# Feed-forward blocks of an encoder trunk: the hand-ordered steps begin at the third pair instead of the fourth, and nine of eleven pairs use seven block products instead of eight

## The chip, the core and the metric

The kernel runs on one core of a Trainium2 chip. A core has five engines, each with its own instruction queue: TensorE (PE in the profile, with its weight loads listed apart as PEld), VectorE (DVE), ScalarE (ACT), GpSimd (POOL) and SyncE (SP), which here only issues DMAs. Engines wait for each other through semaphores. Matmul results go to PSUM, of which this kernel uses eight banks of 128 x 512 fp32; everything else lives in SBUF. The metric is the device time of one launch in microseconds.

## The reference

The reference is a two-layer encoder trunk on 512 tokens of width 1024. Each layer has a feed-forward block, a token mixer (neighbourhood attention in layer 0, a bidirectional RWKV-7 scan in layer 1) and a second feed-forward block, each with a residual and a layer norm. The change touches the four feed-forward blocks only:

```python
def swiglu(x, w_in, w_out):
    gate, up = jnp.split(x @ w_in, 2, axis=-1)
    return (jax.nn.silu(gate) * up) @ w_out

for i in range(DEPTH):                                   # DEPTH = 2
    x = layer_norm(DN_ALPHA * x + 0.5 * swiglu(x, ffn_w_in[i, 0], ffn_w_out[i, 0]), ...)
    ...                                                  # mixer and its norm
    x = layer_norm(DN_ALPHA * x + 0.5 * swiglu(x, ffn_w_in[i, 1], ffn_w_out[i, 1]), ...)
```

`w_in` is 1024 x 5632, `w_out` is 2816 x 1024, all in fp32.

## The kernel before, in words

**Precision.** Every fp32 operand is kept as a high part `h` (rounded to the matmul's format) and a low part `l`. `split` (L278) makes them: ACT copies raw to `h` (L280), DVE or POOL subtracts `h` from raw (L281). A product is three matmuls: h·h, h·l, l·h.

**Tiles of the feed-forward block.** The 2816 hidden columns are NF = 22 tiles of 128, numbered f = 0 to 21, and taken in 11 pairs c: pair c holds f = 2c and f = 2c + 1. For each f there is a gate block and an up block of `w_in`. `ffn` (L465) walks over the pairs; `gated` (L519) makes silu(gate) · up / 2 with one ACT instruction (Silu, L522) and one DVE instruction (L523); `posts` (L525) forms sums and differences of the pair's four quarter tiles with DVE (L529 to L532) and splits them; `sums` (L1128) loads two row tiles of `w_out` and forms sums of them (L1135 to L1140) and splits (tile `wx`); `early` (L1183) multiplies the previous pair's results with these into six PSUM banks (L1206, 18 matmuls of 128 x 512 a pair).

**Two ways to do an input tile.** The plain way is `proj` (L294 with L290 to L292) or, in the hand-ordered part, `plain` (L1065): gate and up, each 8 blocks of 128 input channels by 3 matmuls of 512 columns, 48 matmuls of 128 x 512 for one f. The other way, `products` (L1075), takes gate and up of one f together as a two-by-two block matrix, the tokens' two halves as the other side, and does seven block products in place of eight, Strassen's way in Winograd's form: 7 x 12 = 84 matmuls of 128 x 256. It costs sums on both sides. Those of the weights are made by `weights` (L1013) for each such f with four more DVE instructions (L1040, L1041, L1044, L1048), and eleven half-size splits per pair, seven for the odd f and four for the plain even f. Those of the tokens are made once per block by `mixes` (L944), in four parts, into the four tiles of `right`.

**Which pairs use which.** `SEVEN` (L84) lists the odd f that are done by seven products. A pair whose odd f is in it is built by `slot` (L979), under `manual_schedule` for PE, ACT and DVE: within the slot the instructions of these three engines stand in the order in which the code issues them, and `FF_SEQ` (L86) deals them out among the threads g (plain), s (products), e (early), w (weights), k (posts), u and z (w_out sums). Pairs before that are laid out by the tile scheduler, which picks each engine's order from its own timeline; it may also place scheduled instructions among the first hand-ordered ones. `MIXED` (L85) lists the f after whose `gated` each part of `mixes` is issued.

**What ties the first slot to what stands before it.** All f from 2 on share two PSUM banks, `own` (L933): the gate goes to the first, the up to the second, so the next gate waits for Silu (ACT, L522) to have read the first and the next up waits for L523 (DVE) to have read the second. `prepare` (L994), called while the last plain f before `SEVEN` is projected (L497 to L504), runs the first six steps of `weights`, so that the first slot finds its units. The weights arrive through two `raw` buffers of 128 x 1024; a new load of a buffer waits until the DVE subtraction that last read it is done. All DMAs are issued by SP in one queue.

```python
for c in range(npairs):                                   # ffn, L479
    if 2 * c + 1 in SEVEN:                                # L481
        with self.tc.manual_schedule(engines=MANUAL_SCAN):
            raw = seven.slot(c, out, pool, posts)
    ...
            first = f + 2 == SEVEN[0]                     # L497
            if first:
                seven.prepare(4)
    ...
        if f in MIXED:                                    # L506
            seven.mixes(MIXED.index(f))
```

Of the kernel before, what the change touches and what calls it, by code (L numbers as in the profile page):

```python
# [23 lines left out]
NF = FF // P  # L24
# [56 lines left out]
EARLY_TAGS = ("kz1", "v", "vr", "qc", "qd", "zs", "qs", "tm")  # L81
DECAY = math.exp(-0.5)
GN_EPS = 64e-5
SEVEN = range(7, NF, 2)  # L84
MIXED = (0, 1, 2, 4)  # L85
FF_SEQ = ("g k z u w g w w k g w k g k g s w s w s e e e w s w s s u s s u s s u s e s w s e e w u")  # L86


# [21 lines left out]
class Trunk:  # L110
# [354 lines left out]
    def ffn(self, xT, w_in, w_out, ln, nxt, lead=None):  # L465
# [10 lines left out]
        with self.pool("fa") as pool:  # L476
# [3 lines left out]
            for c in range(npairs):  # L480
                if 2 * c + 1 in SEVEN:  # L481
                    with self.tc.manual_schedule(engines=MANUAL_SCAN):
# [8 lines left out]
                for j in range(2):  # L491
# [3 lines left out]
                    elif not pps:  # L495
                        us = self.units if f == 1 else [self.load_cols(w_in, FF * i + f * P, eng=nc.vector) for i in range(2)]
                        first = f + 2 == SEVEN[0]  # L497
                        if first:
# [6 lines left out]
                    self.gated(pps.pop(0), pps.pop(0), raw[:, 3:7:3] if j else raw[:, 0:8:7])  # L505
                    if f in MIXED:  # L506
                        seven.mixes(MIXED.index(f))
                    if c and j == 0:
# [412 lines left out]
class Seven:  # L921
# [57 lines left out]
    def slot(self, c, out, pool, posts):  # L979

        if 2 * c + 3 not in SEVEN:
            self.work = chain(self.work, out.opening())
# [3 lines left out]
        for name in FF_SEQ.split():  # L986
            next(threads[name], None)
        if 2 * c + 3 not in SEVEN:
            list(out.third(c))
# [23 lines left out]
    def weights(self):  # L1013
# [4 lines left out]
        r = [h for raw in (k.raw(), k.raw()) for h in (raw[:, :512], raw[:, 512:])]  # L1018
        pairs = list(SEVEN)

# [1174 lines left out]
```

## Time and profile before

| | us |
|---|---|
| three runs | 2142.55, 2145.98, 2149.44 (median 2145.98) |
| the profiled execution, its own time | 2143.44 |
| its span, first to last instruction | 2141.7 |
| TensorE clock granted over the span | 0.999 |

The four feed-forward blocks are called FFN0 to FFN3 below. In the profiled execution their first slots begin at 87.6, 671.2, 1018.1 and 1864.5 us from the span's start. In a row of the timeline the first number is the start, the second how long the merged group took, then engine, line, operation, output tile<-input tiles, shape and count; brackets hold the engine's idle time before the row and what ended it. Matmuls overlap, so the step from start to start is the cost of one, not its duration.

### The profile page before, as it was taken

What the parts mean: (1) busy time and instruction counts of PE and PEld (TensorE: products, weight loads), DVE (VectorE), ACT (ScalarE), POOL (GpSimd) and SP (SyncE); (2) the same over time, 40 slices, a digit from 0 to 9 for tenths busy, and PEclk for the clock granted to TensorE, in tenths of its full rate; (3) what the DMA queues carried; (4) which work ended last, traced back from release to release, by engine and by line L of the source; (5) the groups of instructions that cost most, each with busy time, mean ns of one, the idle gap of its engine ahead of it and who ended that gap; (6) DMA issues with size and microseconds to landing.
All of it is one profiled execution on the core that took longest, in us unless ns stands there. A gap on an engine that the chain in (4) does not pass through costs nothing.

```text
span 2141.7 us, 39209 instructions
## 1 busy us (share of the span) xinstructions
PE 2114.4 (99%) x15104; PEld 1715.0 (80%) x15104; DVE 1572.5 (73%) x2678; ACT 1081.1 (50%) x2119; POOL 403.3 (19%) x622
## 2 busy tenths in 40 slices
PE   9999999999999999999999999999999999999998
PEld 8888888888788888888888887535777667788886
DVE  7677776277486777788777779835898658777776
ACT  4444445367443444454444543636888534445443
POOL 1000003455310000020000013043788710000000
PEclk9999999999999999999999999999999999999999
DMA  6544494342334444935444764773454651545474
GB/s 194 186 164 158 158 349 145 111 126 84 99 118 158 158 158 159 388 116 173 138 158 158 276 244 129 270 241 113 115 147 123 223 193 64 169 144 176 169 279 171
DMA packets 180972, 369.44 MB, mean 173 GB/s; under 512 B 34384, under 2 KB 54480, under 8 KB 178736
## 3 DMA queue, kind: packets, MB, share of 16 engines
q1 hardware_dynamic: 180784, 366.94, 50.4%
q8 instruction: 118, 1.93, 0.4%
q14 instruction: 70, 0.57, 0.1%
HBM read 286.13 MB, written 68.68 MB: 166 GB/s over the span
## 4 chain that ended last, share of the span: by engine, by line
PE 77%; DVE 12%; ACT 7%; issue 2%; DMA 1%; POOL 0%; SPq 0%; ACTq 0%; DVEq 0%; POOLq 0%
PE bank L1062 18%; PE bank L1206 17%; PE bank L291 6%; PE bank L290 6%; PE bank L292 5%; PE a L1397 5%; PE bank L353 4%; DVE wx L281 2%; PE g L1723 2%; DVE w L281 1%; ACT ring L280 1%; ACT w L280 1%; PE y L1397 1%; DVE ring L281 1%; PE bank L1590 1%
## 5 line engine op out<-in xcount | busy, mean ns | idle before, releaser
L280 ACT ACTIVATE w<-raw 128x512 fp32r<-128x512 f32 (+1 forms) x302 | 215.0, 727 | 236.9 <-DVE raw L1041 53.9
L1062 PE MATMUL bank<-xT,w 128*128 128x512 f32 (+1 forms) x1572 | 303.2, 347 | 1.3
L1062 PEld LDWEIGHTS bank<-xT,w 128*128 128x128 f32 x1572 | 254.9, 189 | 46.3 <-ACT tmp L522 9.7
L281 DVE TENSOR_TENSOR w<-raw,w 128x512 fp32r<-128x512 f32 (+1 forms) x272 | 206.4, 766 | 86.6 <-ACT w L280 85.5
L447 POOL COPY marks<-x 128x1 f32<-128x1 f32 x8 | 8.2, 1026 | 1039.4 <-DVE x L439 1037.9
L1206 PE MATMUL bank<-wx,an 128*128 128x512 f32 x792 | 200.8, 392 | 0.0
L1206 PE MATMUL bank<-w,ring 128*128 128x512 f32 x720 | 169.2, 390 | 0.0
L280 ACT ACTIVATE ring<-raw 128x512 fp32r<-128x512 f32 (+1 forms) x147 | 102.1, 705 | 119.5 <-DVE raw L1041 37.2
L1206 PEld LDWEIGHTS bank<-wx,an 128*128 128x128 f32 x792 | 142.5, 189 | 24.9
L1206 PEld LDWEIGHTS bank<-w,ring 128*128 128x128 f32 x720 | 135.0, 188 | 29.1 <-DVE w L281 0.3
L290 PE MATMUL bank<-xT,w 128*128 128x512 f32 x368 | 145.1, 394 | 2.4 <-DVE ar L523 2.4
L291 PE MATMUL bank<-xT,w 128*128 128x512 f32 x368 | 143.5, 390 | 0.0
L292 PE MATMUL bank<-xT,w 128*128 128x512 f32 x368 | 142.8, 389 | 0.0
L1062 PE MATMUL bank<-xT,ring 128*128 128x512 f32 (+1 forms) x732 | 140.9, 345 | 0.5
L1062 PEld LDWEIGHTS bank<-xT,ring 128*128 128x128 f32 x732 | 118.0, 189 | 20.4 <-ACT tmp L522 3.8
L1062 PE MATMUL bank<-ring,w 128*128 128x256 f32 x960 | 127.8, 283 | 0.0
L1062 PEld LDWEIGHTS bank<-ring,w 128*128 128x128 f32 x960 | 123.2, 191 | 3.3
L1832 POOL TENSOR_TENSOR tm<-qs,zs 128x126 f32<-128x126 f32 (+22 forms) x248 | 109.6, 442 | 61.4 <-DVE qs L1825 24.0
L1834 POOL TENSOR_TENSOR zs<-zs,tm 128x126 f32<-128x126 f32 (+22 forms) x248 | 108.6, 438 | 19.4
L281 DVE TENSOR_TENSOR ring<-raw,ring 128x512 fp32r<-128x512 f32 (+1 forms) x123 | 85.6, 700 | 25.7 <-ACT ring L280 25.4
L281 DVE TENSOR_TENSOR wx<-ra,wx 128x512 fp32r<-128x512 f32 x132 | 87.2, 686 | 7.5 <-ACT wx L280 4.4
L281 POOL TENSOR_TENSOR w<-raw,w 128x1024 fp32r<-128x1024 f32 x30 | 74.1, 2475 | 86.7 <-ACT w L280 80.7
(386 smaller groups left out, 4555.4 us busy)
## 6 DMA issues: line engine op xcount, KB each, us to landing
raw<-in_ffn_w_in_dram SPq DMA_DIRECT2D x256, 256.0 KB, 3.8
ra<-in_ffn_w_out_dram SPq DMA_DIRECT2D x44, 1024.0 KB, 5.0
raw<-in_ffn_w_in_dram SPq DMA_DIRECT2D x48, 512.0 KB, 3.8
d_away<-away SPq DMA_DIRECT2D x44, 512.0 KB, 4.1
ring<-d_away SPq DMA_DIRECT2D x16, 1024.0 KB, 10.3
xT<-d_late SPq DMA_DIRECT2D x29, 512.0 KB, 9.2
xT<-in_ffn_w_out_dram SPq DMA_DIRECT2D x27, 512.0 KB, 7.9
d_late<-ts SPq DMA_DIRECT2D x44, 256.0 KB, 3.8
```

Of the source, the lines that this page charges most:

```text
L280: self.hi = self.nc.scalar.activation(h, raw, AF.Copy).ins
L281: self.lo = (eng or self.nc.vector).tensor_tensor(l, raw, h.bitcast(F32), ALU.subtract).ins
L290: nc.tensor.matmul(out, wh, xh, start=start, stop=False)
L291: nc.tensor.matmul(out, wh, xl, start=False, stop=False)
L292: nc.tensor.matmul(out, wl, xh, start=False, stop=stop)
L353: nc.tensor.matmul(acc[t, h], a, u[:, i, h * 512 : (h + 1) * 512], start=first and n == 0, stop=last and n == 2)
L1062: self.nc.tensor.matmul(out, w[:, i, cs], x(c)[j], start=start and c + n == 0, stop=stop and c == 3 and n == 2, skip_group_check=True)
L1206: self.nc.tensor.matmul(acc, lhs, u[:, i], start=bool(first) and m == 0, stop=last and m == 2, skip_group_check=more)
L1397: self.nc.tensor.matmul(out[hs], w[:, hs], x, start=start, stop=stop)
L1723: nc.tensor.matmul(pgs[h][:, j * P : (j + 1) * P], flat(bk[hs, q * 4 + j]), ar[hs, :, q * 4 + j], start=True, stop=True)
L1832: nc.gpsimd.tensor_tensor(tv, qs[:, s, 0:s].rearrange("p (a o) -> p a o", o=1).broadcast_to([P, s, n]), zs[:, s : s + 1, c0:].broadcast_to ...
L1834: nc.gpsimd.tensor_tensor(zs[:, 0:s, c0:], zs[:, 0:s, c0:], tv, ALU.add)
```

## The change

`SEVEN` begins at f = 5 instead of 7, so pair 2 (f = 4 and 5) is done by a slot, and there are nine slots instead of eight. The last part of the token mixes is issued after f = 3 instead of f = 4. `prepare` follows by itself: it now runs while f = 3 is projected instead of f = 5.

```diff
-SEVEN = range(7, NF, 2)
-MIXED = (0, 1, 2, 4)
+SEVEN = range(5, NF, 2)
+MIXED = (0, 1, 2, 3)
```

Outside the feed-forward blocks every engine's order is the same as before. FFN1, FFN2 and FFN3 are laid out alike on ACT and DVE; FFN0 differs a little.

**PE in FFN0, from the end of f = 3's gate.** `bank_441` is the gate's bank, `bank_442` the up's; `w_523` and `w_528` are f = 3's gate and up weights; the L1206 rows are the matmuls of `early`. Before, f = 3's up follows its gate at once:

```order
L1206 MATMUL bank_515<-wx_280,an_402 128x512
L292 MATMUL bank_441<-xT_93,w_523 128x512
L290 MATMUL bank_441<-xT_93,w_523 128x512
L291 MATMUL bank_441<-xT_93,w_523 128x512
L292 MATMUL bank_441<-xT_93,w_523 128x512
L290 MATMUL bank_442<-xT_92,w_528 128x512
```

In the changed kernel the first slot's gate matmuls (L1062, weights `ring_260`) stand between them:

```order
L1206 MATMUL bank_514<-wx_280,an_402 128x512
L1206 MATMUL bank_515<-wx_280,an_402 128x512
L1062 MATMUL bank_441<-xT_92,ring_260 128x512 x12
L1062 MATMUL bank_441<-xT_93,ring_260 128x512 x11
L290 MATMUL bank_442<-xT_92,w_528 128x512
```

And where f = 3's up ends, one gate matmul is left before the slot's up (`ring_261`, `w_547`), which writes the same `bank_442`; the 128x256 rows are the first two of the seven products:

```order
L292 MATMUL bank_442<-xT_93,w_528 128x512
L1062 MATMUL bank_441<-xT_93,ring_260 128x512
L1062 MATMUL bank_442<-xT_92,ring_261 128x512 x12
L1062 MATMUL bank_442<-xT_93,w_547 128x512 x12
L1062 MATMUL bank_441<-xT_92,w_547 128x256 x12
L1062 MATMUL bank_441<-ring_256,w_579 128x256 x12
```

What moved: 23 of the slot's first 24 matmuls went ahead of f = 3's up, and the slot's up now stands one matmul behind f = 3's up.

**ACT in FFN0, around the Silu of f = 3** (L522 on `bank_441`, the second L522 row of each piece). Before:

```order
L522 ACTIVATE tmp_491<-bank_441 128x512
L280 ACTIVATE w_528<-raw_527 128x1024
L280 ACTIVATE an_402<-ar_283 128x768
L280 ACTIVATE w_616<-raw_615 128x1024
L280 ACTIVATE away_408<-ar_283 128x2x256
L280 ACTIVATE ring_258<-ring_335 128x1024
L280 ACTIVATE wx_421<-ra_412 128x512
L280 ACTIVATE wx_424<-ra_412 128x512
L280 ACTIVATE wx_427<-ra_412 128x512
L522 ACTIVATE tmp_580<-bank_441 128x512
```

In the changed kernel (`raw_532` and `raw_533` hold the first slot's weights, `ring_258` is the last token mix):

```order
L522 ACTIVATE tmp_491<-bank_441 128x512
L280 ACTIVATE w_528<-raw_527 128x1024
L280 ACTIVATE ring_260<-raw_532 128x512 x2
L280 ACTIVATE an_402<-ar_283 128x768
L280 ACTIVATE ring_261<-raw_533 128x512
L280 ACTIVATE away_408<-ar_283 128x2x256
L280 ACTIVATE w_547<-raw_533 128x512
L280 ACTIVATE w_547<-raw_532 128x512
L280 ACTIVATE ring_258<-ring_335 128x1024
L522 ACTIVATE tmp_609<-bank_441 128x512
```

What moved: the split of f = 4's gate weights (`w_616`) gave way to five half-size splits for the first slot, and the Silu of f = 3 stands behind them and behind the last mix, but ahead of the three `wx` splits.

**DVE in FFN0, up to f = 2's L523** (the reader of `bank_442`). Before:

```order
L281 TENSOR_TENSOR w_528<-raw_527,w_528 128x1024
L955 TENSOR_TENSOR ring_335<-xT_93,xT_92 128x1024
L532 TENSOR_TENSOR ar_283<-ar_283 128x256
L1139 TENSOR_TENSOR ra_412<-ra_412 128x512
L281 TENSOR_TENSOR an_402<-ar_283,an_402 128x768
L957 TENSOR_TENSOR ring_335<-ring_335 128x1024
L281 TENSOR_TENSOR w_616<-raw_615,w_616 128x1024
L1140 TENSOR_TENSOR ra_412<-ra_412 128x512
L281 TENSOR_TENSOR away_408<-ar_283,away_408 128x2x256
L281 TENSOR_TENSOR ring_258<-ring_335,ring_258 128x1024
L523 SCALAR_TENSOR_TENSOR ar_430<-bank_442,tmp_491 128x2x256
```

In the changed kernel, from the mix (L957) on:

```order
L957 TENSOR_TENSOR ring_335<-ring_335 128x1024
L281 TENSOR_TENSOR ring_261<-raw_533,ring_261 128x512
L281 TENSOR_TENSOR away_408<-ar_283,away_408 128x2x256
L1140 TENSOR_TENSOR ra_412<-ra_412 128x512
L281 TENSOR_TENSOR w_547<-raw_533,w_547 128x512
L281 TENSOR_TENSOR w_547<-raw_532,w_547 128x512
L281 TENSOR_TENSOR ring_258<-ring_335,ring_258 128x1024
L523 SCALAR_TENSOR_TENSOR ar_430<-bank_442,tmp_491 128x2x256
```

What moved: one full-size split is gone, and five half-size ones stand ahead of L523, three of them in this piece and two above it, one ahead of L955 and one between L532 and L1139. The last mix (L956, L955, L957) stood ahead of this L523 before as well.

## The prediction

> **What bounds the kernel now.** I read the page's busy shares and clock first, then its chain of waits.
>
> ```profile
> PE 2114.4 (99%) x15104; PEld 1715.0 (80%) x15104; DVE 1572.5 (73%) x2678; ACT 1081.1 (50%) x2119; POOL 403.3 (19%) x622
> PEclk9999999999999999999999999999999999999999
> PE 77%; DVE 12%; ACT 7%; issue 2%; DMA 1%; POOL 0%; SPq 0%; ACTq 0%; DVEq 0%; POOLq 0%
> ```
>
> PE is busy 99% of the span at full clock in every slice, and 77% of the chain is PE work. So the time falls only if PE has less to do, and rises only where PE is made to wait. DVE at 73% is an average, and the change is made where DVE is fuller. Next the windows view, for the first slot of FFN0 and a later one (columns: length, then busy time and count of PE, PEld, DVE, ACT, POOL, then clock, DMA share, GB/s).
>
> ```profile
> 87.61:112.69 25.08, 25.08 (x151) 22.46 (x150) 16.50 (x30) 10.37 (x20) 0.00 (x0) 1.00 0.38 127
> 125.35:150.79 25.44, 25.36 (x153) 22.38 (x151) 20.10 (x34) 12.31 (x25) 0.00 (x0) 1.00 0.48 168
> ```
>
> Inside a slot PE never stands still for long: 25.36 of 25.44 us busy, with DVE at 20.10 and ACT at 12.31. A slot is thus worth its matmuls, and the prices come from the timeline of PE in FFN0.
>
> ```profile
> 72.65 4.24 PE L1206 MATMUL bank<-wx,an 128*128 128x512 f32 x18
> 76.73 0.39 PE L290 MATMUL bank<-xT,w 128*128 128x512 f32 x1
> ...
> 87.61 8.32 PE L1062 MATMUL bank<-xT,ring 128*128 128x512 f32 x36
> ...
> 99.92 1.60 PE L1062 MATMUL bank<-ring,w 128*128 128x256 f32 x12
> 101.36 2.23 PE L1206 MATMUL bank<-wx,an 128*128 128x512 f32 x9
> ...
> 112.69 2.88 PE L1062 MATMUL bank<-xT,ring 128*128 128x512 f32 x12
> ...
> 125.35 1.60 PE L1062 MATMUL bank<-ring,w 128*128 128x256 f32 x12
> ```
>
> From 76.73 to 87.61 stand one plain f's 48 matmuls of 512 columns: 10.88 / 48 = 0.2267 us a step. Twelve of 256 columns go from 99.92 to 101.36: 0.120 us a step. Eighteen `early` matmuls take 76.73 - 72.65 = 4.08 us. A slot takes 112.69 - 87.61 = 25.08 us the first time and 125.35 - 99.92 = 25.43 from the same place to the same place of the next.
>
> **The PE work that the change swaps.** In each FFN pair 2 is now 96 + 18 matmuls of 512 columns, 114 x 0.2267 = 25.84 us. It becomes a slot. FFN0's first slot stays the only kind without a boundary before it, so the added one is a steady slot, 25.43 us. Gain 0.41 us per FFN, **1.64 us** in four. By steps alone it would be more: 48 x 0.2267 = 10.88 us go and 84 x 0.120 = 10.08 come, 0.80 us per FFN or 3.2 in all. The measured slot keeps half of that, and a row of the waits view of PEld says where most of the other half stays.
>
> ```profile
> PEld bank L1062 <- ACT tmp L522: 13.5, 28, 0.5
> ```
>
> 28 waits are seven boundaries in each of four FFNs: at each, the next pair's first products wait for Silu to leave the shared bank (in the start times a boundary is some 0.24 us longer than its matmuls). Nine slots have eight boundaries, so four more of these waits come; they are in the 25.43 already. I take 1.64, the measured end, and keep 3.2 as the other.
>
> The 256-column price deserves doubt, because each of these matmuls loads 128 columns of weights for half as many steps.
>
> ```profile
> L1062 PEld LDWEIGHTS bank<-ring,w 128*128 128x128 f32 x960 | 123.2, 191 | 3.3
> ```
>
> Spread over its count a load is 123.2 / 960 = 0.128 us, as long as the 0.120 us step: 84 x 0.128 = 10.75 us against 10.88 saved. If loads set the step under a fuller slot, the swap is worth 0.13 us per FFN instead of 0.80; that is the lower end. It is not what the steady slots show.
>
> [...]
>
> **The join in FFN1 to FFN3.** What stands ahead of the first slot decides whether it starts on time. PE's timeline shows one stop there in FFN0 and one in each later FFN, in the waits view together:
>
> ```profile
> PE bank L290 <- DVE ar L523: 2.4, 4, 0.7
> ```
>
> ```profile
> 55.30 0.39 PE L292 MATMUL bank<-xT,w 128*128 128x512 f32 x1
> 56.19 0.50 PE L290 MATMUL bank<-xT,w 128*128 128x512 f32 x1 [0.51 <-DVE ar L523]
> ...
> 649.39 0.61 PE L292 MATMUL bank<-xT,w 128*128 128x512 f32 x2
> 650.65 0.47 PE L290 MATMUL bank<-xT,w 128*128 128x512 f32 x1 [0.65 <-DVE ar L523]
> ```
>
> In FFN1 the two matmuls from 649.39 would let the next start at 649.84; it starts at 650.65, **0.81 us** late. The up of f = 4 waits there for the L523 of f = 3, which can only begin when f = 3's up is done, one matmul before. In the changed kernel the up of f = 4 belongs to the slot, and again one matmul (the slot's last gate one) lies between. The stop stays as it is: no gain, no cost, if DVE comes to that L523 in time. Whether it does:
>
> ```profile
> 636.66 1.22 DVE L281 TENSOR_TENSOR w<-raw,w 128x1024 fp32r<-128x1024 f32 x1 [0.59 <-ACT w L280]
> 637.80 0.68 DVE L523 SCALAR_TENSOR_TENSOR ar<-bank,tmp 128x512 f32<-128x512 f32 x1
> 638.40 1.22 DVE L957 TENSOR_TENSOR ring<-ring 128x1024 f32<-128x1024 f32 x1
> ...
> 646.63 0.69 DVE L1135 TENSOR_TENSOR ts<-ra 128x512 f32<-128x512 f32 x1 [3.74 <-DMA ra<-in_ffn_w_out_dram]
> ...
> 649.82 0.69 DVE L523 SCALAR_TENSOR_TENSOR ar<-bank,tmp 128x512 f32<-128x512 f32 x1 [1.04 <-PE bank L292]
> ```
>
> ```profile
> 649.86 1.06 ACT L280 ACTIVATE w<-raw 128x1024 fp32r<-128x1024 f32 x1 [8.98 <-issue]
> ```
>
> Between the L523 of f = 2 (637.80) and that of f = 3 (649.82) DVE idles 3.74 + 1.04 us, and 0.59 just before. `prepare` puts about ten half-size operations of 512 columns there, each a step of 0.60 (637.80 to 638.40): +6.0 us; two full-size splits (1.14 each, from 636.66 to 637.80) and three half-size ones go or move behind: -4.1. Net +2.0 us, and some 1.5 more where a split on DVE waits for its half on ACT. That fits into 5.4 with 1.9 us left. ACT, idle for 8.98 us ahead of its 649.86 row, has room. I cost it at **zero**. The cover ends if weights come late, since four more DMAs of 256 KB stand in SP's queue ahead of the 1 MB load of `w_out`:
>
> ```profile
> ACT ring L280 <- DMA raw<-in_ffn_w_in_dram: 22.7, 16, 4.2
> ACT w L280 <- DMA raw<-in_ffn_w_in_dram: 32.7, 30, 1.9
> ```
>
> The longest such wait is 4.2 us and the mean 22.7 / 16 = 1.4. A mean one is covered by 1.9; the longest overruns it by 2.3 us.
>
> **The join in FFN0.** Here DVE has no idle time at all, so the same question is put to ACT's and DVE's rows.
>
> ```profile
> 46.78 1.21 DVE L281 TENSOR_TENSOR w<-raw,w 128x1024 fp32r<-128x1024 f32 x1
> 47.91 1.21 DVE L955 TENSOR_TENSOR ring<-xT 128x1024 f32<-128x1024 f32 x1
> 49.05 0.41 DVE L532 TENSOR_TENSOR ar<-ar 128x256 f32<-128x256 f32 x1
> 49.38 0.67 DVE L1139 TENSOR_TENSOR ra<-ra 128x512 f32<-128x512 f32 x1
> ...
> 50.86 1.21 DVE L957 TENSOR_TENSOR ring<-ring 128x1024 f32<-128x1024 f32 x1
> ...
> 53.13 0.67 DVE L1140 TENSOR_TENSOR ra<-ra 128x512 f32<-128x512 f32 x1
> ...
> 55.47 0.67 DVE L523 SCALAR_TENSOR_TENSOR ar<-bank,tmp 128x512 f32<-128x512 f32 x1
> ```
>
> ```profile
> 52.10 1.06 ACT L280 ACTIVATE ring<-ring 128x1024 fp32r<-128x1024 f32 x1 [1.97 <-DVE ring L957]
> ...
> 55.72 0.60 ACT L522 ACTIVATE tmp<-bank 128x512 f32<-128x512 f32 x1
> ```
>
> ```profile
> raw<-in_ffn_w_in_dram SPq DMA_DIRECT2D x256, 256.0 KB, 3.8
> ```
>
> The slot's gate needs f = 3's Silu (L522) to have emptied the first bank. PE could start it at about 55.5: all of f = 3's gate and 18 `early` matmuls lie ahead of it, as many as before the 55.30 row. On ACT that Silu now stands behind five half-size splits and the last mix. The fifth splits a block whose buffer is freed by DVE's second new split. That one stands behind L955 and L532 and one more new split: 47.91 + 0.60 + 1.14 + 0.33 + 0.60 = 50.6. The load lands 3.8 us later, 54.4; then the half split (0.6), the mix's split (0.96, a 1.06 row less its overlap) and Silu (0.5) end at 56.5. PE is then **1.0 us** late. With a landing of 3.3 us it is 0.5, and with the mix alone (L957, at 50.86, moves back by two half splits, 1.2, and ends at 53.2, so ACT is through at 54.9) nothing is lost: ends 0 and 1.3, value 1.0. It takes the place of the stop at 56.19 (56.19 - 55.30 - 0.23 = 0.66 us), because f = 3's up now comes 23 matmuls later and its L523 is long done: +0.3. Then the slot's up waits for the L523 of f = 3 as in FFN1, about +0.8, which FFN0 did not have in that place before. FFN0 pays +1.1.
>
> The last mix costs nothing: its three DVE steps were already ahead of the 55.47 row, at 47.91 and behind it. At a block's end nothing is added to PE's queue, and the DMA bytes are the same.
>
> **Sum.** -1.64 + 0.3 + 0.8 = -0.54 us. The profiled execution took 2143.44 us (span 2141.7) and would take 2142.9; on the median of the three runs, 2145.98, that is **2145.4**. A measurement of this kernel tells 0.3%, 6.4 us, from no change; the runs shown alone spread from 2142.55 to 2149.44.
>
> **Rivals.**
>
> *The stops vanish (0.08).* If the L523 stop fell away in all four FFNs, 2.4 to 3.2 us would go on top of 1.64: about 2141. For it: 23 of the slot's matmuls now stand ahead of f = 3's up. Against it: the slot's up still follows that up by one matmul. With 3.2 for the swap as well it is 2139.6, still no more than 0.3% faster: nothing in these rows can give 6.4 us, which is why I hardly allow for it.
>
> *The weights are late (0.07), slower.* The place is DVE between the two L523 of FFN1 to FFN3 and ACT's Silu in FFN0. From the point where a weight block lands more than 1.9 us late, DVE reaches the L523 of f = 3 after PE has finished its up, and every us goes to PE. At the longest wait seen, 2.3 us each in three FFNs and as much in FFN0 make 9; less the swap's gain about +7.5, 2153.5. For it: four more loads in one queue ahead of the `w_out` load for which DVE already waits 3.74 us. Against it: the mean wait is 1.4.
>
> *The swap saves nothing (0.03).* Loads set the narrow step: 4 x 0.13 = 0.5 gained, 1.1 paid, 2146.6.
>
> *Several small stops (0.06).* The FFN0 stall at 1.3 and stalls of 0.5 to 1 us where a unit is split just in time: +1.5 to +5, 2147 to 2151.
>
> **How the numbers follow.** The forecast (2144 to 2147 in its mechanism) has 0.76. The range adds the spread of the runs shown and leaves out the late weights and the far end of the vanishing stops: 2140.5 to 2150.5. Faster by over 0.3%: 0.03, for what I may have overlooked. Slower: 0.06, nearly all of it the late weights. Within: 0.91.
>
> **What would show it.** In the profile of the changed kernel: 15104 + 4 x 36 = 15248 matmuls; 32 waits of L1062 for L522 in place of 28; steady slots still at 25.4 us; first slots about 25 us sooner; a stop of 0.8 us at the slot's up in every FFN; in FFN0 a stop of about 1 us ahead of the slot's gate, ended by ACT L522. Wrong would be: a stop of PE of more than 2 us at the join, DVE idle there on ACT and ACT on `raw` (late weights); slots of another length (the price of the narrow matmul); or no stop at the slot's up.

## The result: slower by 18 us, and the profile after

| | us |
|---|---|
| before, four runs | median 2146.34 (2142.55 to 2149.44) |
| changed, four runs | median 2164.21 (2161.1 to 2166.36) |
| ratio, 95% interval | 1.0089 (1.0077 to 1.0101) |
| profiled execution, changed | 2166.36, span 2164.0, granted clock 0.995 |

The kernel became 0.9% slower where 2145.4 was forecast, and the time lies outside the range. First the page and the waits view of PE in the changed kernel (in a waits row: total us, times, longest).

```profile
PE 2122.6 (98%) x15248; PEld 1723.9 (80%) x15248; DVE 1598.2 (74%) x2734; ACT 1093.6 (51%) x2167; POOL 404.2 (19%) x622
```

```profile
PE bank L1206 <- DVE w L281: 12.1, 4, 3.1
...
PE bank L1062 <- DVE ar L523: 2.2, 4, 0.6
...
PE bank L1062 <- ACT tmp L522: 1.1, 4, 0.4
```

The first row of the waits is new: four stops of 3.1 us, one in each feed-forward block. L1206 is not the first slot's line; it is the line of the products with `w_out`, and these stops stand at each **block's end**, behind the last slot. Here is that place in FFN0, PE's timeline, first before, then after.

```profile
304.33 8.54 PE L1206 MATMUL bank<-w,ring 128*128 128x512 f32 x36
```

```profile
304.61 6.05 PE L1206 MATMUL bank<-w,ring 128*128 128x512 f32 x26
313.72 4.63 PE L1206 MATMUL bank<-w,ring 128*128 128x512 f32 x10 [3.06 <-DVE w L281]
```

The same 36 matmuls run through before and are cut after the 26th. And the ten behind the stop take 4.63 us, where ten steps of 0.2267 are 2.3. DVE's rows at that place, before and after, show what PE waits for:

```profile
302.49 5.46 DVE L560 SCALAR_TENSOR_TENSOR x<-x,bank 128x512 f32<-128x512 f32 x9
307.87 1.22 DVE L281 TENSOR_TENSOR wl<-xT,wl 128x1024 fp32r<-128x1024 f32 x1
309.00 1.22 DVE L281 TENSOR_TENSOR w<-xT,w 128x1024 fp32r<-128x1024 f32 x1
310.14 2.47 DVE L560 SCALAR_TENSOR_TENSOR x<-x,bank 128x512 f32<-128x512 f32 x4
```

```profile
304.13 3.68 DVE L560 SCALAR_TENSOR_TENSOR x<-x,bank 128x512 f32<-128x512 f32 x6 [1.79 <-PE bank L1206]
307.73 1.22 DVE L281 TENSOR_TENSOR wl<-xT,wl 128x1024 fp32r<-128x1024 f32 x1
308.86 3.67 DVE L560 SCALAR_TENSOR_TENSOR x<-x,bank 128x512 f32<-128x512 f32 x6
312.44 2.36 DVE L281 TENSOR_TENSOR w<-xT,w 128x1024 fp32r<-128x1024 f32 x2
```

L560 adds finished banks into the residual `x`; nothing near waits for the six that stand between the two splits. The L281 row on `w` is the low half of the first tile of the next group of products (`t3`, c = 0), and PE cannot go on without it. Before, nine L560 stand ahead of the two splits; after, six, then one split, then six more, then the split that PE needs. PE finishes the banks for the first three later than before (DVE idles 1.79 us ahead of its L560 row), so the first split comes at the same time, 307.7 instead of 307.9, and the second one six L560 later. Nothing else kept it: ACT had made its half from 306.17 on.

```profile
306.17 1.06 ACT L280 ACTIVATE w<-xT 128x1024 fp32r<-128x1024 f32 x1 [1.83 <-PE bank L1206]
```

The windows view of the changed kernel explains the 4.63 us (length, then busy time and count of PE, PEld, DVE, ACT, POOL, then the granted clock, DMA share, GB/s): the stretch behind each of the four stops.

```profile
313.72:319.60 5.88, 5.88 (x14) 4.62 (x15) 4.69 (x8) 1.06 (x1) 0.00 (x0) 0.50 1.02 420
902.82:908.70 5.88, 5.88 (x19) 4.67 (x20) 5.17 (x8) 1.06 (x1) 0.00 (x0) 0.71 1.02 421
1254.62:1260.50 5.88, 5.88 (x19) 4.69 (x20) 5.17 (x8) 1.06 (x1) 0.00 (x0) 0.71 0.99 396
2108.22:2114.10 5.88, 5.88 (x19) 4.71 (x20) 5.18 (x8) 1.06 (x1) 0.00 (x0) 0.71 1.00 408
```

At 0.2267 us a step 5.88 us hold 26 matmuls. There are 14, 19, 19 and 19, that is 33 too few, worth 7.5 us: behind the stop the granted clock was 0.50 for some microseconds (for all of the first row, for part of the others, whose mean is 0.71). The page's row of the clock in 40 slices still reads 9 throughout; a slice is 54 us.

So of the 22.3 us between the two spans 12.1 are the stops and 7.5 the half clock. The scan in layer 1 took 2.65 more (rows below, first before, then after), and that leaves nothing. The scan's instructions are the same in both. Among the runs below it took 544.71 in e1, which has nine slots and the old order at the block's end, and 544.04 in e2, which has eight slots and the new order, so neither the ninth slot nor that order makes these 2.65; the execution before has the shortest scan of all that were profiled.

```profile
1286.69:1827.71 541.02, 533.79 (x6234) 349.06 (x6233) 398.71 (x721) 314.13 (x760) 248.31 (x514) 1.00 0.51 161
```

```profile
1302.34:1846.01 543.67, 535.05 (x6235) 349.06 (x6233) 400.11 (x722) 315.12 (x763) 248.49 (x514) 1.00 0.52 161
```

### The profile page after: what moved, and what is told of

Read it like the earlier page. It is cut to its first block, busy times and chain, and to the rows that moved or that the text cites. A ratio compares the mean times of both kernels' runs of the same rounds, so it can differ in the third digit from the quotient of the medians.

```text
span 2164.0 us, 39660 instructions
## 1 busy us (share of the span) xinstructions
PE 2122.6 (98%) x15248; PEld 1723.9 (80%) x15248; DVE 1598.2 (74%) x2734; ACT 1093.6 (51%) x2167; POOL 404.2 (19%) x622
## 4 chain that ended last, share of the span: by engine, by line
PE 72%; DVE 14%; ACT 8%; issue 4%; DMA 2%; SPq 0%; ACTq 0%; DVEq 0%
PE bank L1062 19%; PE bank L1206 15%; PE a L1397 5%; PE bank L291 4%; PE bank L290 4%; PE bank L292 4%; PE bank L353 4%; DVE wx L281 2%; DVE w L281 2%; ACT w L280 2%; PE g L1723 2%; ACT ring L280 1%; PE y L1397 1%; DVE ring L281 1%; DVE x L560 1%
## 5 line engine op out<-in xcount | busy, mean ns | idle before, releaser
L1062 PE MATMUL bank<-xT,w 128*128 128x512 f32 (+1 forms) x1728 | 332.4, 346 | 1.7 <-ACT tmp L522 0.6
L1062 PEld LDWEIGHTS bank<-xT,w 128*128 128x128 f32 x1728 | 279.7, 189 | 50.0 <-ACT tmp L522 10.1
L281 DVE TENSOR_TENSOR w<-raw,w 128x512 fp32r<-128x512 f32 (+1 forms) x288 | 209.3, 734 | 96.5 <-ACT w L280 96.1
L1206 PE MATMUL bank<-wx,an 128*128 128x512 f32 x792 | 202.3, 392 | 0.0
L1206 PE MATMUL bank<-w,ring 128*128 128x512 f32 x720 | 176.3, 402 | 12.1 <-DVE w L281 12.1
L1206 PEld LDWEIGHTS bank<-w,ring 128*128 128x128 f32 x720 | 139.5, 194 | 43.9 <-DVE w L281 13.8
L1062 PE MATMUL bank<-xT,ring 128*128 128x512 f32 (+1 forms) x864 | 169.4, 347 | 3.6 <-DVE ar L523 2.2
L280 ACT ACTIVATE ring<-raw 128x512 fp32r<-128x512 f32 (+1 forms) x159 | 108.7, 699 | 109.8 <-DVE raw L1041 37.4
L1062 PEld LDWEIGHTS bank<-xT,ring 128*128 128x128 f32 x864 | 139.3, 189 | 30.3 <-ACT tmp L522 6.8
L1206 PEld LDWEIGHTS bank<-wx,an 128*128 128x128 f32 x792 | 141.8, 189 | 24.2
L1062 PE MATMUL bank<-ring,w 128*128 128x256 f32 x1152 | 153.7, 283 | 0.2
L1062 PEld LDWEIGHTS bank<-ring,w 128*128 128x128 f32 x1152 | 147.7, 191 | 5.0 <-ACT tmp L1082 1.0
L281 DVE TENSOR_TENSOR ring<-raw,ring 128x512 fp32r<-128x512 f32 (+1 forms) x135 | 93.4, 701 | 28.5 <-ACT ring L280 28.3
L290 PE MATMUL bank<-xT,w 128*128 128x512 f32 x256 | 101.1, 395 | 0.0
L291 PE MATMUL bank<-xT,w 128*128 128x512 f32 x256 | 99.9, 390 | 0.0
L292 PE MATMUL bank<-xT,w 128*128 128x512 f32 x256 | 99.6, 390 | 0.0
L281 DVE TENSOR_TENSOR wx<-ra,wx 128x512 fp32r<-128x512 f32 x132 | 87.1, 688 | 6.9 <-ACT wx L280 3.9
L281 POOL TENSOR_TENSOR w<-raw,w 128x1024 fp32r<-128x1024 f32 x30 | 74.1, 2476 | 87.1 <-ACT w L280 80.6
```

The lines of the kernel that those rows point to most:

```text
L280: self.hi = self.nc.scalar.activation(h, raw, AF.Copy).ins
L281: self.lo = (eng or self.nc.vector).tensor_tensor(l, raw, h.bitcast(F32), ALU.subtract).ins
L290: nc.tensor.matmul(out, wh, xh, start=start, stop=False)
L291: nc.tensor.matmul(out, wh, xl, start=False, stop=False)
L292: nc.tensor.matmul(out, wl, xh, start=False, stop=stop)
L1062: self.nc.tensor.matmul(out, w[:, i, cs], x(c)[j], start=start and c + n == 0, stop=stop and c == 3 and n == 2, skip_group_check=True)
```

## What ties the block's end to the number of slots

Each slot needs 11 units of split weights, made by `weights`. `spots` deals them out in turn to **nine places**: two in the tile `pair`, one in `one`, two in each of three `w` tiles, A, B and C.

```python
tiles = [lambda: k.sb_w.tile([P, 2 * D], F32R, name="w", tag="w", bufs=k.nw) for _ in range(3)]
for t in (lambda: self.pair, None, *tiles):        # L1006: pair, one, A, B, C
```

There are only three `w` buffers, and the tiles that the block's end needs (two from `opening`, then those of `load`) take them over, in the programs as built, in the order in which they come free. Eight slots use 88 units: the last one falls on place 87 mod 9 = 6, in B. Nine use 99, and the last one falls on 98 mod 9 = 8, in C. Count the last slot's units from 1 to 11. With eight slots its `w` tiles are read for the last time with units 4 (C), 9 (A) and 11 (B); with nine, with units 7 (A), 9 (B) and 11 (C). So the second and the third new tile find their buffer where they found it before, but the first has to wait for unit 7 instead of unit 4. The traces of FFN0 show it in ACT's first full-size split of `opening`, before, then after:

```profile
280.14 1.06 ACT L280 ACTIVATE w<-raw 128x1024 fp32r<-128x1024 f32 x1
```

```profile
283.15 1.06 ACT L280 ACTIVATE w<-raw 128x1024 fp32r<-128x1024 f32 x1 [2.89 <-issue]
```

The order behind the last slot is the scheduler's, and it came out differently on DVE, ACT, PE and SP. **Theory A**: this turn of the places changes the order on DVE at the block's end, and the order costs the time. **Rival B**: the ninth slot itself, with fuller DVE, SP and DMA, delays the end. **Rival C**: a `w` buffer really comes free too late, and the order only follows.

## The experiments

The second line of the change, `MIXED` alone, moves no row on any engine: the scheduler had the last mix in that place already. So there is no run of it, and all that follows is about `SEVEN`.

**e1: nine slots, places turned.** The changed kernel with one `w` tile listed first, so that the last slot reads its three `w` tiles for the last time with units 4, 9 and 11 again, as with eight slots.

```diff
-        for t in (lambda: self.pair, None, *tiles):
+        for t in (tiles[2], lambda: self.pair, None, *tiles[:2]):
```

> Nine slots as in the changed kernel; only the list of the nine places for units in spots is turned, so that one w tile comes first and the other two last, and the last slot leaves its w tiles in the same phase as eight slots did. In the build the rows of DVE at each block's end then stand as before the change. Theory A (the time is lost because the phase in which 99 units instead of 88 leave the nine places makes the scheduler put six L560 ahead of the split of the first t3 tile on DVE): the wait of L1206 for DVE w (12.1 us in four) is gone, the clock stays full, and the time is that of before less the small gain of the swap: 2143 to 2147 where before is 2146, ratio 0.998 to 1.001. Rival B (the ninth slot itself, with its fuller DVE, SP and DMA, delays the block's end): the waits stay, about 2164, ratio 1.008. Rival C (a w buffer really comes free too late, the order on DVE only follows): fast as with A.

Measured: 2145.03 beside 2145.39 before, ratio 0.9998 (0.9989 to 1.0007). The waits view has no row of L1206 for DVE any more, and DVE stands as before the change:

```profile
302.49 5.46 DVE L560 SCALAR_TENSOR_TENSOR x<-x,bank 128x512 f32<-128x512 f32 x9
307.87 1.22 DVE L281 TENSOR_TENSOR wl<-xT,wl 128x1024 fp32r<-128x1024 f32 x1
309.00 1.22 DVE L281 TENSOR_TENSOR w<-xT,w 128x1024 fp32r<-128x1024 f32 x1
```

Its first split of `opening` starts at 280.08 again. The scan in the windows view, of e1 and then of e2:

```profile
1285.91:1830.62 544.71, 536.49 (x6235) 350.38 (x6233) 399.48 (x722) 315.30 (x763) 248.94 (x514) 1.00 0.52 160
```

```profile
1299.01:1843.05 544.04, 535.86 (x6234) 349.78 (x6233) 400.18 (x721) 314.53 (x760) 248.48 (x514) 1.00 0.52 160
```

All of the loss is gone with the ninth slot still there, so rival B falls.

**e2: eight slots, places turned the other way.** The kernel before, with its places in the phase of the changed one: last reads with units 7, 9 and 11. Its first split of `opening` starts at 283.32.

```diff
-        for t in (lambda: self.pair, None, *tiles):
+        for t in (None, *tiles, lambda: self.pair):
```

> The kernel before, eight slots, with the places in spots turned so that its 88 units leave the w tiles in the phase that 99 leave them in in the changed kernel; DVE's rows at a block's end then stand as in the changed kernel. Theory A: four waits of about 3.1 us of L1206 for DVE w and about 2.9 us of half clock behind each, 4 x 6 = 24 us on top of before: 2168 to 2171, ratio 1.010 to 1.012. Rival B (it takes the ninth slot): 2146, ratio 1.000. Rival C: slow as with A.

Measured: 2165.14, ratio 1.0093 (1.0079 to 1.0106). The whole loss of the change appears without the change. Its waits view has the row of the changed kernel again, 12.1 us in four of at most 3.1, and so has PE's timeline in FFN0:

```profile
313.90 2.57 PE L1206 MATMUL bank<-w,ring 128*128 128x512 f32 x10 [3.06 <-DVE w L281]
```

The stop in FFN0 is as long as in the changed kernel, yet its ten matmuls take 2.57 us: in this execution two of the four stops were followed by half clock, two were not. The profiled execution was the quickest of four (2162.38, mean granted clock 0.997; the others 0.994 to 0.996), so missing half clock need not be the whole reason why the median lies 3 us under what was expected.

**e3: only the order on DVE.** The changed kernel, buffers and places untouched; the last six L560, and the two for V that follow, are kept behind the split (`behind` makes what is issued inside it follow the named instruction on its engine).

```diff
+            with self.behind(out.opened):       # DVE's half of t3, c = 0
                 for t in (2, 3):
                     more(t, 1, X)
                     more(t, 0, X, ALPHA)
...
```

> The changed kernel with its places and its buffers as they are; only the last six L560 ahead of the V ones are kept behind DVE's split of the first t3 tile in ffn_out. Theory A: that split then starts when ACT's half is done (309.9 in FFN0 of the changed kernel) and PE, which is ready at 310.5, waits about 0.5 us instead of 3.1, at full clock: heads as in the changed kernel, 2144 to 2149, ratio 0.999 to 1.002. Rival C (the buffer comes free late): the wait stays at about 3 us, 2164, ratio 1.008. Rival B: 2164 as well.

Measured: 2146.35, ratio 1.0006 (0.9997 to 1.0015). DVE, then PE, in FFN0:

```profile
308.02 1.22 DVE L281 TENSOR_TENSOR wl<-xT,wl 128x1024 fp32r<-128x1024 f32 x1
309.15 1.22 DVE L281 TENSOR_TENSOR w<-xT,w 128x1024 fp32r<-128x1024 f32 x1
310.29 3.67 DVE L560 SCALAR_TENSOR_TENSOR x<-x,bank 128x512 f32<-128x512 f32 x6
...
304.90 8.32 PE L1207 MATMUL bank<-w,ring 128*128 128x512 f32 x36
```

The 36 matmuls run through again (the edits shift L1206 by a line or two here and below). I had expected a stop of 0.5 us, having taken the wrong one of ACT's splits for this tile's; the right one is done by 307.2 in the changed kernel, and nothing stops. With the same buffers, the same phase and the changed orders ahead of this place on all engines the loss is gone, so rival C falls too: it is DVE's order alone.

**e4, e5, e6: how long a stop costs how much.** Three, five, or more instructions let through ahead of the split. In e4 and e5:

```diff
+            adds = [(2, 1, X), (2, 0, X, ALPHA), (3, 1, X), (3, 0, X, ALPHA), (0, 0, X, ALPHA), (1, 0, X, ALPHA)]
+            for a in adds[:3]:                  # e5: adds[:5]
+                more(*a)
             with self.behind(out.opened):
...
```

In e6 the DVE half of the split itself (`late_low`; ACT's half stays where it was) is put behind the first L560 of V:

```diff
-                more(t, 0, V, 1.0, st[t][0])
+                last = more(t, 0, V, 1.0, st[t][0])
+                if t == 0:
+                    with self.behind(last):
+                        out.late_low()
```

> As e3, with three of the six L560 let through ahead of that split: the wait should be 0.6 to 1.3 us, 0.2 to 0.75 more than in e3 in each block. Theory A1 (a short stop costs itself only, a stop of 3 us also halves the granted clock for some 6 us): 1 to 3 us over e3, clock 0.999. Rival A2 (any stop of a microsecond halves the clock behind it): 4 x (0.5 + 2.9) = 14 us over e3, clock 0.996.

> As e4, with five of the six L560 let through: the wait of L1206 for DVE w should be about 1.3 + 2 x 0.6 = 2.5 us in each block, 4.8 us over e4 in four. Theory A1 as it now stands (stops of 1.3 us left the clock full, those of 3.1 halved it behind four of four in the changed kernel and two of four in e2): if the limit lies above 2.5, the time is e4 plus 4.8, 2156, ratio 1.005, and every matmul behind the stop steps at 0.23 us. If the limit lies below, 1.7 to 2.9 us more behind each, 2163 to 2168.

> The changed kernel with the DVE half of that split moved further back still, behind the first L560 of V: one full split and one L560 more ahead of it, 1.1 + 0.6 us, so stops of about 4.8 us in place of 3.1. Theory A1: every one of the four stops is followed by a stretch at half clock that costs 1.7 to 2.9 us: 4 x (4.8 + 1.7 to 2.9) = 26 to 31 us over e3, 2172 to 2177, ratio 1.012 to 1.015. Rival A3 (the half clock has nothing to do with the length of the stop but with the state of the chip): some stops without it, as in e2, 2166 to 2172.

Waits (total, times, longest) of e4, e5 and e6, in this order:

```profile
PE bank L1208 <- DVE w L281: 5.0, 4, 1.3
```

```profile
PE bank L1208 <- DVE w L281: 9.8, 4, 2.5
```

```profile
PE bank L1209 <- DVE w L1240: 20.2, 4, 5.8
```

And windows behind a stop: one of e4, one of e6, two of e5.

```profile
312.10:318.00 5.90, 5.90 (x26) 4.90 (x27) 5.90 (x9) 2.68 (x3) 0.00 (x0) 1.00 1.03 392
```

```profile
315.36:320.60 5.24, 5.24 (x12) 4.12 (x13) 2.82 (x4) 0.53 (x1) 0.00 (x0) 0.50 1.01 413
```

```profile
901.16:905.20 4.04, 4.04 (x11) 3.19 (x12) 4.04 (x6) 0.00 (x0) 0.00 (x0) 0.58 1.03 419
2103.76:2108.00 4.24, 4.24 (x18) 3.46 (x19) 4.24 (x6) 1.06 (x1) 0.00 (x0) 1.00 0.99 407
```

| | stops, us each | followed by half clock | median us | ratio to before (95%) |
|---|---|---|---|---|
| e3 | none | | 2146.35 | 1.0006 (0.9997 to 1.0015) |
| e4 | 1.3 | 0 of 4 | 2151.55 | 1.0030 (1.0019 to 1.0042) |
| e5 | 2.5 | 3 of 4 | 2161.09 | 1.0077 (1.0063 to 1.0091) |
| e2 | 3.1 | 2 of 4 | 2165.14 | 1.0093 (1.0079 to 1.0106) |
| changed | 3.1 | 4 of 4 | 2164.21 | 1.0089 (1.0077 to 1.0101) |
| e6 | 4.8 to 5.8 | 4 of 4 | 2176.10 | 1.0146 (1.0132 to 1.0160) |

The third column counts the profiled execution alone. e4 costs what its stops last: 5.2 us over e3 for 5.0 of waits. I had expected 1 to 3, because I took stops of 0.5 us for e3, which has none. Rival A2, at 14 us, falls. From e4 to e5 the waits grow by 4.8 and the time by 9.5. e6 costs 29.8 over e3 for 20.2 of waits. I had expected e5 at 2156, or at 2163 to 2168; at 2161 it stands between, with half clock behind three stops of four. So the length of a stop does not decide alone. Rival A3 holds in part: for stops of 2.4 to 3.1 us something besides the length has a say, and the last section has what the rows show of it.

**e7: a version for use.** e1's rows left one thing at the join: the slot's up still waits for f = 3's L523 (0.56 us in FFN1 to FFN3; in FFN0 e1 is laid out otherwise than the changed kernel and keeps the stop of before, 0.7 us at f = 3's up). e7 is e1 with the first slot kept behind the last matmul of f = 3's up on PE, so that the slot's whole gate lies between the two ups:

```diff
-                    with self.tc.manual_schedule(engines=MANUAL_SCAN):
+                    with self.tc.manual_schedule(engines=MANUAL_SCAN), self.behind(*(self.upend,) if 2 * c + 1 == SEVEN[0] else ()):
```

> e1 (nine slots, places turned, full clock at the blocks' ends) with the first slot also kept behind the last matmul of f = 3's up on PE, so that the slot's whole gate, 24 matmuls or 5.4 us, lies between that up and the slot's up, which writes the same bank. If the stop of L1062 for DVE ar L523 (0.56 us idle, three in e1) comes only from the two ups standing one matmul apart, it is gone in FFN1 to FFN3 and the heads are 1.7 us shorter: about 2 us below e1 and 2 to 4 us below before in the FFNs, ratio 0.998 to 0.9995, which five rounds may just tell from 1. Rival: the slot's units, planned later, arrive late instead, and a stop for ACT or DVE of 0.5 to 3 us stands ahead of the slot in each FFN: ratio 1.000 to 1.004.

Measured: 2141.1 beside 2145.12 before, ratio 0.9981 (0.9972 to 0.9990): faster than either kernel, and 0.19% under before. It lies 3.7 us under e1, each taken against its own runs of before, where 2 were expected. FFN1's join, PE's timeline of e1 and then of e7:

```profile
650.59 7.21 PE L1062 MATMUL bank<-xT,ring 128*128 128x512 f32 x36 [0.56 <-DVE ar L523]
```

```profile
645.00 5.60 PE L1062 MATMUL bank<-xT,w 128*128 128x512 f32 x24
650.44 7.04 PE L1062 MATMUL bank<-xT,ring 128*128 128x512 f32 x36
```

The bracket is gone. FFN1 from its first `early` matmul to its last product, in the windows view of before, of e1 and of e7:

```profile
634.88:872.75 237.87, 236.65 (x1350) 207.01 (x1349) 179.43 (x298) 110.69 (x208) 0.00 (x0) 1.00 0.50 172
```

```profile
634.91:872.37 237.46, 236.21 (x1387) 207.97 (x1386) 185.70 (x311) 112.95 (x217) 0.00 (x0) 1.00 0.51 174
```

```profile
635.48:871.92 236.44, 235.86 (x1386) 208.09 (x1385) 185.20 (x311) 112.74 (x217) 0.00 (x0) 1.00 0.51 173
```

The swap as such takes 237.87 - 237.46 = 0.41 us off this stretch in e1, the freed join 1.02 more, of which the stop itself is 0.72 from start to start. At the block's end e7 has two stops, in FFN0 and FFN1, that e1 has not:

```profile
PE bank L1206 <- DVE w L281: 1.2, 2, 0.7
```

FFN0 is ordered alike in both; there ACT waited 3.53 us for its DMA where it had waited 2.77 in e1. The place has no slack: before the change the split ends at 310.1 for matmuls due at 310.2.

## Why the prediction was wrong

**The step that failed** is the sentence "At a block's end nothing is added to PE's queue, and the DMA bytes are the same." It holds word for word, and it was used to price the block's end at zero. Nothing was added; what changed was the order there, some 220 us behind the edited slot, because the count of units moved the turn of the places. DVE's order alone cost four stops of 3.1 us (12.1) and 7.5 us of half clock behind them. The orders that I laid side by side were those of the join. A row-by-row comparison behind the last slot would have shown the six L560 ahead of the split, and the trace of before would have priced them: six L560 at 0.60 us is 3.6 us, on a split that starts there at 309.00, takes 1.14 and is due at 310.2 (304.33 and 26 steps), so a stop of some 3.5 us; 3.1 came. None of the rivals had its place at the block's end, so the range could not hold the time.

**The half clock** was not in any term either. The trace of before shows it only at its very end, from 2136.29 us, where PE has been idle since its last matmul ended at 2131.99; its longest stop ahead of that, 1.88 us at 1395.08, left the clock at 1.00.

**The swap**, 0.41 us per FFN, was right as a price: FFN1 shows 0.41 in e1, and a steady slot of the changed kernel still takes 25.43 us.

```profile
112.70:138.13 25.43, 25.34 (x151) 22.38 (x150) 20.09 (x35) 12.34 (x24) 0.00 (x0) 1.00 0.46 166
```

The price of the narrow matmul was right with it. The matmul count is 15248 as written, and the waits of L1062's weight loads for L522 are 33 where 32 were said. But in the changed kernel itself the gain did not arrive. The same stretch of FFN1 takes 0.28 us more than before there:

```profile
640.45:878.60 238.15, 236.47 (x1386) 208.04 (x1385) 185.00 (x310) 111.79 (x215) 0.00 (x0) 1.00 0.50 172
```

Two stops of PE for L522 within this stretch, 0.37 and 0.20 us, which e1 does not have, are most of the difference to e1. Over the four blocks these stretches take 953.90 us in the changed kernel, 953.54 before and 951.64 in e1. So ahead of the block's end the changed kernel lost 0.36 us where a gain of 0.54 was forecast: the rival of several small stops came true in small.

**The join in FFN1 to FFN3** was right in kind: the weights came in time, and the slot's up stops for L523 in all four blocks, 0.56 us idle by the waits where about 0.8 from start to start was said (0.72 measured).

**The join in FFN0** was right in place and too dear in size: PE stops for ACT's Silu ahead of the slot's gate, 0.31 us, not 1.0. The rows of ACT show the chain as predicted, shorter:

```profile
53.63 0.64 ACT L280 ACTIVATE w<-raw 128x512 fp32r<-128x512 f32 x1 [1.63 <-DMA raw<-in_ffn_w_in_dram]
54.17 1.04 ACT L280 ACTIVATE ring<-ring 128x1024 fp32r<-128x1024 f32 x1
55.12 0.57 ACT L522 ACTIVATE tmp<-bank 128x512 f32<-128x512 f32 x1
...
55.75 5.51 PE L1062 MATMUL bank<-xT,ring 128*128 128x512 f32 x23 [0.31 <-ACT tmp L522]
```

The fifth half split starts at 53.63, not 54.4: DVE's second new split ends at about 50.4 where 50.6 was said, and the block lands some 3.2 us behind it, not the median of 3.8.

Without the block's end the time would have lain inside the range. e3, which keeps the joins and slots of the changed kernel, is 1.0 us above before (-0.6 to 3.2), and e1 is 0.4 under (-2.4 to 1.5 us). Neither can tell the sum of -0.5 us from nothing.

**What stays open** is which step of the scheduler's own plan makes it put six L560 ahead of the split when the first `w` buffer comes free three units later. That the turn decides it is shown from both sides (e1, e2), and that the order alone costs the time by e3; how the plan gets there was not looked into.

## What to carry to other kernels

A count that runs through a ring of buffers leaves the ring in another phase, and whatever takes over the buffers, far behind the edit, can be ordered anew: compare the orders to the end of the stage, on every engine, and price each row that passed another. In a kernel that PE bounds, a stop of some microseconds is to be priced with the slow stretch that may follow: here 12.1 us of stops brought 7.5 us more. And where an order made by a scheduler turns out bad, one ordering edge at the row that is waited for (e3, e7) mends it without giving up the change.

## What the runs showed of the clock

Behind single stops of PE the granted clock fell to 0.50: after none of four stops of 1.3 us (e4), three of four of 2.5 (e5), six of eight of 3.1 (e2 and the changed kernel), all four of 4.8 to 5.8 (e6). Apart from these stretches the changed kernel's clock is recorded at 1.00 from 5.59 us up to 2159.40; from there it is 0.50 to the end, and the last matmul had ended at 2154.74.

The times at which the clock changes show where the stops of e2 differ. In the changed kernel it falls at 312.79, 903.30, 1254.87 and 2108.20 us; the distances, 590.51, 351.57 and 853.33, are 173, 103 and 250 times 3.413. In e2 it falls at 899.80 and 1251.38, again 103 such steps apart. Here are stretches of this length around two stops of e2, both 3.06 us long; that they lie so in FFN0 too, where the clock does not change, is an estimate, counted 172 steps back from the fall in FFN1:

```profile
309.29:312.70 3.41, 1.55 (x7) 0.94 (x5) 3.41 (x7) 2.84 (x3) 0.00 (x0) 1.00 1.04 410
312.71:316.12 3.41, 2.22 (x10) 1.84 (x11) 3.41 (x5) 0.00 (x0) 0.00 (x0) 1.00 1.02 414
896.39:899.80 3.41, 0.35 (x2) 0.21 (x2) 3.41 (x6) 1.74 (x2) 0.00 (x0) 1.00 1.03 405
899.81:903.21 3.40, 3.40 (x9) 2.65 (x9) 3.40 (x5) 0.00 (x0) 0.00 (x0) 0.50 1.05 430
903.23:906.63 3.40, 3.40 (x16) 2.77 (x16) 2.16 (x4) 1.15 (x2) 0.00 (x0) 1.00 0.99 402
```

In FFN0 PE is idle for 1.86 us of one stretch and 1.19 of the next, and the clock stays; in FFN1 it is idle for 3.06 of one, and the next one runs at 0.50. In the changed kernel PE is idle for 2.13, 2.94, 3.08 and 2.94 us of the 3.41 ahead of the four falls. That the place of a stop decides was not shown by itself, since no run moved a stop of the same length, and these rows give no limit. The changed kernel's four executions took 2161.1 to 2166.36 us at mean clocks of 0.997 to 0.995.

The slow stretch lasts 3.41 us behind three stops of the changed kernel and 6.83 behind that of FFN0; behind the stops of e6 the mean clock is 0.50 or 0.51 over windows of 5.2 to 6.1 us. In the changed kernel matmuls of 512 columns step at 0.427 us in it, in place of 0.2267. Counted as matmuls too few in the windows above, at 0.2267 us each, a slow stretch cost 1.5 to 2.7 us.
